# One channel block of a depthwise convolution: band products on TensorE against multiplies on ScalarE and sums on GpSimd

## Chip, cores, metric

The kernel runs on one core of a Trainium2 chip. The metric is the device time of one execution in microseconds. The names of the profile are PE (TensorE matmuls), PEld (TensorE weight loads), DVE (VectorE), ACT (ScalarE), POOL (GpSimd) and SP (SyncE, which issues the DMAs).

## What is computed

A decoder trunk of two layers over 1024 tokens of 1024 channels, all in 32-bit floats. The first layer mixes tokens with a gated causal depthwise convolution, the second with sliding-window attention; each is followed by a layer norm, a squared-ReLU MLP, another layer norm and a gated embedding. The part that matters here is the convolution:

```python
CONV_WIDTH = 31
h = x @ w_in + b_in
a, gate = jnp.split(h, 2, axis=-1)
h = a * jax.nn.sigmoid(gate)
h = lax.conv_general_dilated(          # each channel by itself: 31 taps, causal
    h, w_dw[:, None, :], window_strides=(1,), padding=[(CONV_WIDTH - 1, 0)],
    dimension_numbers=("NWC", "WIO", "NWC"), feature_group_count=D_MODEL) + b_dw
h = jax.nn.silu(layer_norm(h, ln_g, ln_b))
return h @ w_out + b_out
```

## The kernel before

Every product of two matrices is made of three TensorE products: each operand is split into a high part, rounded to a shorter format (fp32r) by a ScalarE cast, and a low remainder, formed by VectorE (`split`, `mm3`). Names ending in h and l (wh, wl, xh, xl) are these parts.

The convolution stage fills roughly the first 260 us and works by eight channel blocks of 128 channels (`c` = 0 to 7). Two generators are advanced in turn. `conv_in(c)` makes x @ w_in for the block, four steps each: it puts the sum into PSUM, takes the sigmoid of the gate on ScalarE, multiplies on VectorE and hands the gated block over to DRAM (`hand_over`, tensors zz and scr). Blocks 2 to 6 use a product with seven in place of eight parts (`conv_seven`), whose token forms T[1] to T[4] are made by `forms()` and `last_forms()`. `taps(c)` starts `LAG` = 6 steps later. It loads the block back from scr with tokens dealt into four phases (a B tile), loads the tap weights as band matrices (z, from w_dw), casts each to high and low halves (an E tile, by ScalarE and VectorE), and multiplies: per E tile nine products of 128x128 by 128x256, one for each shift. Two such tiles make a step, eight a block. The bias is added by ScalarE and the low half by VectorE (tile g), the sums are transposed on TensorE (ps slots of the kind `tr`), and the result of blocks 0 to 5 is stored to the DRAM tensor `kept`; the tiles Z[half, phase, q] (slots X and A, one for each of eight token tiles and each half of the channels) are filled from it when block 6 comes. Then `conv_ln` takes pairs of token tiles: statistics, normalization, transposition, Silu. While these last steps run, products of the embedding are woven in (`fill`). The output projection `mix_out` with w_out follows.

The order of the instructions on each engine is fixed ahead by a planner, `Recorder.schedule`. Each operation has a number by its place in the program (moved back by `later`), an estimated duration (`cost`), and is put on its engine when its operands and slots are ready, the lowest number first. `after` makes an operation wait for another; `slack` adds to the estimated ready time. Buffers come from small pools of slots by name, six PSUM slots for ps and two for tr. The planner's estimate for an addition on GpSimd is `90.0 + 2.2 * f` ns for f elements per partition; for an activation on ScalarE it is `60.0 + f * 0.85`, plus 90 for a bias pointer and 130 for a scale pointer. It also lets VectorE operations with two SBUF inputs and GpSimd operations exclude each other in time (`held`).

Of the kernel before, what the change touches and what calls it, by code (L numbers as in the profile page):

```python
# [10 lines left out]
F32 = mybir.dt.float32  # L11
F32R = mybir.dt.float32r
AF = mybir.ActivationFunctionType
ALU = mybir.AluOpType

P = 128
T = 1024
D = 1024
KB = D // P
NT = T // P  # L20
HT = 512
TAPS = 31
NH = 16
# [9 lines left out]
PH = 4  # L33
# [5 lines left out]
U = T // PH  # L39
LO = 288  # L40
LAG = 6
SC = 144
ROWS = slice(0, P // 2), slice(P // 2, P)
WAIT = 250.0
# [9 lines left out]
KEPT = 6  # L54
# [458 lines left out]
class Emit:  # L513
# [320 lines left out]

    def setup(self):
        nc, d = self.nc, self.d
        self.cc = self.const("cst", (P, 256 + NT * 32 + 2 * NH), F32)[:, 0 : 32 + 64]
        self.ident = self.const("ident", (P, P), F32)
        self.mhalf = self.const("mhalf", (P, 32), F32)[:, 0:1]
        nc.gpsimd.memset(self.mhalf, -0.5)  # L840

        self.xT = {}
        for k in ((0, 0), (0, 1), (1, 0), (1, 1)):
            for p in "hl":
                nc.slots(f"x{p}{k[0]}{k[1]}", [f"x{p}{k[0]}{k[1]}"])
            self.xT[k] = self.xT_quarter(k)
# [19 lines left out]
    def conv(self):  # L866

        nc, d, ws = self.nc, self.d, self.ws
        cc = self.cc
        ba, bg, lg, lb = (cc[:, 8 * i : 8 * i + 8] for i in range(4))  # L870
        bdw = cc[:, 32:96]
        HIGH, LOW = slice(0, P // 2), slice(P // 2, P)

        self.warm_up()
# [7 lines left out]
        Z = {}  # L882

        def hand_over(c, h, g):

            both = self.sb("wh" if (c, h) == (LAST, 1) else "zz", F32R, 2 * HT)
            self.split(g, both[:, 0:HT], both[:, HT : 2 * HT])
            if c not in scr:
                scr[c] = nc.tile(f"scr{c}", (2 * PH * P, U), F32, "DRAM")
            cols = slice(h * P, (h + 1) * P)  # L890
            dst = scr[c].scatter(lambda a: a.rearrange("(k q) u -> q k u", q=P)[:, :, cols], P, cols, 2 * PH)
            nc.sync.dma_start(dst, both.bitcast(F32).rearrange("p (k u) -> p k u", k=2 * PH))

        T = {j: [None] * 4 for j in range(1, 5)}
# [83 lines left out]
        def conv_in(c):  # L978

            if ALONE <= c < LAST:  # L980
                yield from conv_seven(c)
                return
            us = ws.get(2)
            if c == LAST:
                for kb in range(KB // 2):
                    self.load_xT(1, kb)
            for h in (0, 1) if c in (0, LAST) else (1, 0):
                pp = [self.ps() for s in range(2)]
                order = [(kb + KB // 2 * (h if c == LAST else 0)) % KB for kb in range(KB)]

                def part(s, kb):
                    wh, wl = us[kb // 4]
                    o = (kb % 4) * 256 + (1 - s) * P
                    tr = [(wh[:, o : o + P], wl[:, o : o + P], *self.xs(kb, h * HT, HT))]
                    self.mm3(pp[s], tr, kb == order[0], kb == order[-1])

                if c == 0:
                    for kb in range(KB):
                        part(0, kb)
                        part(1, kb)  # L1000
                    yield
                else:
                    for s in range(2):
                        for kb in order:
                            part(s, kb)
                        if s == 0:
                            yield
                sg = self.sb("t")
                nc.scalar.activation(sg, pp[0], AF.Sigmoid, bias=bg[:, c : c + 1], scale=1.0)
                g = self.sb("t")  # L1010
                nc.vector.scalar_tensor_tensor(
                    out=g, in0=pp[1], scalar=ba[:, c : c + 1], in1=sg, op0=ALU.add, op1=ALU.mult
                )
                hand_over(c, h, g)
                yield
            ws.done(2)

        exchange = None

        def taps(c):  # L1020

            n = SHIFTS * PH * CG
            nonlocal exchange
            for jj in range(2):
                pss = [self.ps() for k in range(2)]
                for j in range(2):
# [4 lines left out]
                    src = scr[c].scatter(  # L1031
                        lambda a, pair=pair: a.rearrange("(k p j) u -> (k p) j u", p=CG, j=NG)[:, pair, :], P, slice(0, U), 2
                    )
                    nc.sync.dma_start(G2[:, :, HIST : HIST + U], src)
                    exchange = nc.ops[-1]
                    for k in range(2):
                        w = nc.tile("z", (P, n))
                        nc.sync.dma_start(w, d["w_dw"][c, jj, 2 * j + k])
                        w = w.rearrange("p (m q) -> p m q", q=PH * CG)
# [3 lines left out]
                        if e in fresh:  # L1043
# [4 lines left out]
                            out=ev[HIGH, :, 1, :], in0=w[HIGH], in1=ev[HIGH, :, 0, :].bitcast(F32), op=ALU.subtract  # L1048
                        )
                        for i in range(SHIFTS):  # L1050
                            o = k * LO + HIST - i
# [6 lines left out]
                y = self.sb("g")  # L1058
                for k in range(2):
                    r = slice(k * P // 2, (k + 1) * P // 2)  # L1060
                    for j in range(2):
                        half = slice(j * U, (j + 1) * U)
                        b = 4 * c + 2 * jj + j
# [5 lines left out]
                pt = self.ps("tr")  # L1069
                pv = pt.rearrange("p (h f j k q) -> p h j k f q", h=2, f=PH, j=2, k=2)  # L1070
                nc.slack = SLACK
                for h in range(2):
                    for j in range(2):
                        o = h * P + j * U
                        nc.tensor.transpose(pv[:, h, j], y[:, o : o + P], self.ident)
                nc.slack = 0.0
                if c < KEPT:
                    for h in range(2):
                        if jj == 0:
                            wait[h] = self.sb("t")  # L1080
                        v = wait[h].rearrange("p (f j u) -> p f j u", f=PH, j=2)
                        src = pt[:, h * 256 : (h + 1) * 256].rearrange("p (f u) -> p f u", f=PH)
                        (nc.scalar.copy if h else nc.vector.tensor_copy)(v[:, :, jj, :], src)
                        if jj:
                            dst = kept.rearrange("p (s c u) -> p s c u", s=2 * PH, c=KEPT)
# [3 lines left out]
                if c == KEPT and jj == 0:  # L1089
                    for q in range(2):  # L1090
                        m = min(4, KEPT - 4 * q)
                        for h in range(2):
                            for f in range(PH):
                                Z[h, f, q] = self.sb("XA"[q])
                                o = ((PH * h + f) * KEPT + 4 * q) * P
                                with nc.later(BACK_BY):
                                    nc.sync.dma_start(Z[h, f, q][:, 0 : P * m], kept[:, o : o + P * m])
                for h in range(2):
                    for f in range(PH):
                        o = c % 4 * P + jj * 4 * CG  # L1100
                        dst = Z[h, f, 1][:, o : o + 4 * CG]
                        src = pt[:, (PH * h + f) * 4 * CG : (PH * h + f + 1) * 4 * CG]
# [42 lines left out]
        kept = self.dram("kept", 2 * KEPT * HT)  # L1145
        wait = {}
        stores = []
        ins = (x for c in range(8) for x in conv_in(c))
        outs = (x for c in range(8) for x in taps(c))
        for n in range(32 + LAG):  # L1150
            next(ins, None)
            if n >= LAG:
                next(outs, None)
            if n == 32:
                idle = (x[:, k, :] for q in (1, 0) for x in self.xT_quarter((q, 1), F32) for k in range(4))
                fill = self.embed(0, (0, 1), idle, lambda *v: stores.append(v))
            for k in range(WOVEN[n - 32] if n >= 32 else 0):
                next(fill)
        for g in (ins, outs):
            assert next(g, LAG) == LAG  # L1160


        with nc.later(EMBED_BY[0]):
# [10 lines left out]
        nc.move("ps", "tr")  # L1174
        with nc.after(exchange):
            gb = self.load_row("g", d["mix_g"][0:1]), self.load_row("g", d["mix_b"][0:1])
            ws.add(*[d["w_out"][0, u] for u in range(4)])
            ws.pump()
        marks = []
        for t in range(0, NT, 2):  # L1180
            conv_ln(t)
# [731 lines left out]
    def scores(self, n, g, qf):  # L1913
# [14 lines left out]

        s = nc.tile("z", (P, 4 * SC)).rearrange("p (h s) -> p h s", h=4)
        with nc.after(qf) if n == 0 else contextlib.nullcontext():  # L1930
# [118 lines left out]
def layout(a):  # L2049
    c = np.ascontiguousarray  # L2050
# [7 lines left out]
    p = np.asarray(a["p"])[:, 0]  # L2058
    r = {}
# [3 lines left out]
    r["pT"] = c(np.stack([p[0][phased], p[1]]).transpose(0, 2, 1).reshape(2, 2, P, T))  # L2063
    wi = np.asarray(a["conv_w_in"])[0]
    chan = np.arange(P).reshape(NG, CG).T.ravel()
    r["w_in"] = c(wi.reshape(2, 4, P, 2, 8, P)[..., chan].transpose(4, 0, 2, 1, 3, 5).reshape(8, 2, P, 1024))

    w2 = wi[:, np.concatenate([np.arange(D, 2 * D), np.arange(D)])].reshape(8, P, 2, 8, P)[..., chan]
    r["w_in2"] = c(w2.transpose(3, 2, 1, 0, 4).reshape(8, 2, P, 1024)[ALONE:])
# [1 line left out]
    def cm(v):  # L2071
        return v.reshape(8, P).T

    bi = np.asarray(a["conv_b_in"])[0]
    wd = np.asarray(a["conv_w_dw"])[0]
# [6 lines left out]
    for q in range(CG):  # L2082
# [5 lines left out]
    r["cconst"] = c(  # L2088
        np.concatenate(
            [  # L2090
                cm(bi[:D])[chan], cm(bi[D:])[chan],
                cm(np.asarray(a["conv_ln_g"])[0]), cm(np.asarray(a["conv_ln_b"])[0]),
                np.tile(bd, (2 * PH, 1)),
            ],
            axis=1,
        )
    )
    own = np.tril(np.ones((P, P), np.float32))
    mask = np.concatenate([own, own.T], axis=1)
    f = np.float32(THETA) ** (-np.arange(0, ROPE, 2, dtype=np.float32) / np.float32(ROPE))  # L2100
# [16 lines left out]
    wd = np.asarray(a["mlp_w_down"]).reshape(2, 8, 2, 2, P, 2, HT)  # L2117
# [16 lines left out]
```

## Time and profile before

| | |
|---|---|
| median of 3 runs | 2127.36 us (2126.59 to 2128.29) |
| profiled execution, its own time | 2126.79 us |
| span of the profile | 2124.6 us |
| granted TensorE clock | 0.999 |
| band products (ps<-B,E, 128x256) | 576 |
| instructions on GpSimd | 494 |

The page gives the busy share of every engine and the chain of work that ended last. The view by stretches gives the same for any part of the span; the view by groups puts together instructions of one engine, operation and shape, with busy time, mean duration and the idle time before them; the timeline lists instructions in order of time, where "x4" stands for four of one kind in a row, with the time from the first one's start to the last one's end. All source lines are L480, a helper's, so that instructions are told apart by their tiles.

### The profile page before, as it was taken

To read this page: it belongs to the slowest core of one execution; us is meant where nothing else is said; L and a number is where in the kernel's file an instruction comes from. 1 tells how busy PE (TensorE), PEld (TensorE's weight loads), DVE (VectorE), ACT (ScalarE), POOL (GpSimd) and SP (SyncE) were. 2 spreads that over 40 slices of the span, in tenths; PEclk is the share of its full clock that TensorE was granted. 3 is DMA by queue.
4 is the path that set the end of the run, shared out by engine and by line. 5 is a ranking of instruction groups with operands and counts; after the bars stand their busy time and mean duration, and the time that the engine had idled before them with its cause. 6 is when DMAs were issued, how large, how long until landed. Compare 5 with 4: busy or idle time off the path is not lost.

```text
span 2124.6 us, 29630 instructions
## 1 busy us (share of the span) xinstructions
PE 2110.1 (99%) x9984; PEld 1749.8 (82%) x9984; DVE 1688.8 (79%) x2692; ACT 1211.9 (57%) x2271; POOL 265.5 (12%) x494
## 2 busy tenths in 40 slices
PE   9999999999999999999999999999999999999998
PEld 7888888888888888888888878887888888888887
DVE  8767698987777879876976888698787768788688
ACT  6655654766566533344656888366666663333373
POOL 0000114100000000002131656150000000000041
PEclk9999999999999999999999999999999999999999
DMA  7768964887787757564586112677877785574735
GB/s 258 235 213 285 290 202 151 290 268 249 263 263 262 262 157 249 184 197 155 174 305 220 48 54 93 216 248 246 273 260 262 269 310 174 184 247 164 244 110 203
DMA packets 220760, 463.99 MB, mean 218 GB/s; under 512 B 22208, under 2 KB 55616, under 8 KB 220608
## 3 DMA queue, kind: packets, MB, share of 16 engines
q1 hardware_dynamic: 220608, 462.11, 64.9%
q8 instruction: 78, 1.28, 0.2%
q14 instruction: 74, 0.61, 0.1%
HBM read 314.96 MB, written 147.06 MB: 217 GB/s over the span
## 4 chain that ended last, share of the span: by engine, by line
PE 86%; DVE 6%; ACT 3%; DMA 3%; issue 1%; POOL 1%; SPq 0%; DVEq 0%; POOLq 0%; ACTq 0%
PE ps L480 66%; PE tr L480 20%; ACT z L480 2%; DVE z L480 1%; DMA raw<-in_w_up_dram 1%; DVE t L480 1%; DVE g L480 1%; DVE sm L480 1%; POOL sm L480 1%; DVE wl L480 1%; DVE B L480 1%; DVE E L480 0%; DMA wh<-gate_t 0%; DVE xl L480 0%; DMA hid<-zz 0%
## 5 line engine op out<-in xcount | busy, mean ns | idle before, releaser
L480 PE MATMUL ps<-xh 128*128 128x512 f32 x618 | 240.4, 389 | 0.0
L480 PE MATMUL ps<-xl,xh 128*128 128x512 f32 x618 | 240.4, 389 | 0.0
L480 PE MATMUL ps<-xh,xl 128*128 128x512 f32 x618 | 240.4, 389 | 0.0
L480 POOL TENSOR_SCALAR sm<-sm 128x1 f32<-128x1 f32 x72 | 26.4, 370 | 1371.3 <-DVE E L480 609.2
L480 PE MATMUL ps<-xh,wh 128*128 128x512 f32 x496 | 193.6, 394 | 1.9 <-ACT z L480 1.9
L480 PE MATMUL ps<-xl,wh 128*128 128x512 f32 x496 | 194.4, 392 | 0.0
L480 PE MATMUL ps<-xh,wl 128*128 128x512 f32 x496 | 194.1, 392 | 0.0
L480 ACT CAST wh<-raw 128x1024 fp32r<-128x1024 f32 (+2 forms) x134 | 119.4, 895 | 92.8 <-PE ps L480 65.6
L480 ACT CAST xh<-wh 128x1024 fp32r<-128x1024 f32 x76 | 79.7, 1049 | 119.0 <-PE ps L480 81.2
L480 DVE TENSOR_TENSOR wl<-raw,wh 128x1024 fp32r<-128x1024 f32 (+2 forms) x100 | 97.9, 981 | 54.3 <-ACT wh L480 53.9
L480 PEld LDWEIGHTS ps<-xh,xl 128*128 128x128 f32 x618 | 116.0, 188 | 24.2
L480 PEld LDWEIGHTS ps<-xl,xh 128*128 128x128 f32 x618 | 116.0, 188 | 24.1
L480 PEld LDWEIGHTS ps<-xh 128*128 128x128 f32 x618 | 116.0, 188 | 23.9
L480 ACT CAST wh<-g 128x512 fp32r<-128x512 f32 x136 | 81.0, 619 | 92.9 <-PE ps L480 61.0
L480 PE MATMUL ps<-wh,xh 128*128 128x512 f32 (+1 forms) x304 | 119.1, 392 | 0.6 <-DMA wh<-gate_t 0.6
L480 PE MATMUL ps<-wl,xh 128*128 128x512 f32 (+1 forms) x304 | 119.2, 392 | 0.0
L480 PE MATMUL ps<-wh,xl 128*128 128x512 f32 (+1 forms) x304 | 119.1, 393 | 0.0
L480 DVE TENSOR_TENSOR wl<-g,wh 128x512 fp32r<-128x512 f32 x136 | 90.0, 688 | 34.7 <-ACT wh L480 34.5
L480 ACT ACTIVATE t<-t 128x512 f32<-128x512 f32 x144 | 91.0, 632 | 44.1 <-DVE t L480 42.2
L480 PEld LDWEIGHTS ps<-xh,wh 128*128 128x128 f32 x496 | 93.6, 189 | 22.5 <-ACT z L480 2.3
L480 PEld LDWEIGHTS ps<-xh,wl 128*128 128x128 f32 x496 | 93.6, 189 | 19.6
L480 PEld LDWEIGHTS ps<-xl,wh 128*128 128x128 f32 x496 | 93.8, 189 | 18.4 <-DVE xl L480 0.5
(418 smaller groups left out, 5748.3 us busy)
## 6 DMA issues: line engine op xcount, KB each, us to landing
wh<-hid SPq DMA_DIRECT2D x78, 512.0 KB, 4.3
raw<-in_w_up_dram SPq DMA_DIRECT2D x68, 512.0 KB, 4.3
wl<-in_w_down_dram SPq DMA_DIRECT2D x58, 512.0 KB, 4.8
hid<-zz SPq DMA_DIRECT2D x96, 256.0 KB, 4.8
z<-in_w_dw_dram SPq DMA_DIRECT2D x64, 288.0 KB, 4.0
hid<-t SPq DMA_DIRECT2D x64, 256.0 KB, 4.8
raw<-hid SPq DMA_DIRECT2D x30, 512.0 KB, 4.1
hid<-z SPq DMA_DIRECT2D x36, 256.0 KB, 4.9
```

What stands on the lines that cost most here:

```text
L480: getattr(getattr(nc, o.eng), o.name)(*a, **k)
```

## The change

Channel block 0 (`OWN`) leaves the band path. Its input weights are kept in the natural order of channels, its gated values stay in natural token order in a B tile (`own`; the second token half is stored to the DRAM tensor `own_g` and loaded into a second B tile when needed), and for each of two token halves and two pairs of phases, 31 ScalarE activations multiply the shifted tokens by one tap each (the first adds the bias), into two buffers in turn; GpSimd adds them up. The four results are transposed on TensorE; two go to `kept` as before, and the two of the second half are copied from PSUM directly into their Z tiles, whose loads then leave out block 0's columns. The multiplies are recorded from step 11 on at 4.75 to a step. In addition, the four loads of w_out are put in as two pairs, the second 70 numbers later.

```diff
+OWN = 0
+OWN_FROM, OWN_RATE = 11, 4.75
+OWN_LAST = (1, 0), (1, 2)
+OWN_LAG, OWN_ASK, OWN_NEXT = 6, 22, 12
+OWN_SLACK = 3000.0
+OUT_BY = 70
...
     def conv(self):
...
-                g = self.sb("t")
+                if c == OWN:
+                    if h == 0:
+                        own[0] = nc.tile("B", (P, 2 * LO))
+                        g = own[0][:, TAPS - 1 : TAPS - 1 + HT]
+                    else:
+                        g = self.sb("t")
+                    rows, g = g, g.rearrange("p (u f) -> p f u", f=PH)
+                    sg, pp[1] = (v.rearrange("p (f u) -> p f u", f=PH) for v in (sg, pp[1]))
+                else:
+                    g = self.sb("t")
                 nc.vector.scalar_tensor_tensor(
                     out=g, in0=pp[1], scalar=ba[:, c : c + 1], in1=sg, op0=ALU.add, op1=ALU.mult
                 )
-                hand_over(c, h, g)
+                if c == OWN:
+                    if h == 0:
+                        nc.gpsimd.memset(own[0][:, 0 : TAPS - 1], 0.0)
+                    else:
+                        own[1] = self.dram("own_g", HT)
+                        nc.sync.dma_start(own[1], rows)
+                else:
+                    hand_over(c, h, g)
...
+        def taps_alone():
+            n = PH // 2 * P
+            acc, part = self.sums[:, 0:n], nc.tile("z", (P, 2 * LO))
+            part = [part[:, k * n : (k + 1) * n] for k in range(2)]
+            pend = []
+            def give(h, f, y):
+                pt = self.transpose4([y[:, k * P : (k + 1) * P] for k in range(2)], OWN_SLACK)[:, 0:n]
+                if (h, f) in OWN_LAST:
+                    for k, copy in enumerate((nc.vector.tensor_copy, nc.scalar.copy)):
+                        copy(Z[h, f + k, 0][:, OWN * P : (OWN + 1) * P], pt[:, k * P : (k + 1) * P])
+                    return
+                v = self.sb("t")[:, 0:n]
+                nc.scalar.copy(v, pt)
+                dst = kept.rearrange("p (s c u) -> p s c u", s=2 * PH, c=KEPT)
+                nc.sync.dma_start(dst[:, PH * h + f : PH * h + f + 2, OWN, :], v.rearrange("p (f u) -> p f u", f=2))
+            for h in range(2):
+                near = own[h]
+                for f in range(0, PH, 2):
+                    for i in range(TAPS):
+                        src = near[:, i : i + HT].rearrange("p (u f) -> p f u", f=PH)[:, f : f + 2, :]
+                        w = own_taps[:, i : i + 1]
+                        out = part[i % 2] if i else acc
+                        bias = dict(bias=own_bias) if i == 0 else {}
+                        with nc.after(T[3][3][1]) if (h, f, i) == (0, 0, 0) else contextlib.nullcontext():
+                            nc.scalar.activation(out.rearrange("p (f u) -> p f u", f=2), src, AF.Identity, scale=w, **bias)
+                        if i:
+                            if i == OWN_ASK:
+                                pend.append((h, f, self.sb("g")[:, 0:n]))
+                            to = acc if i < TAPS - 1 else pend[0][2]
+                            nc.gpsimd.tensor_tensor(out=to, in0=acc, in1=out, op=ALU.add)
+                        yield
+                        if (h, f, i) == (0, 2, OWN_NEXT):
+                            half, own[1] = own[1], nc.tile("B", (P, 2 * LO))
+                            nc.scalar.copy(own[1][:, 0 : TAPS - 1], near[:, HT : HT + TAPS - 1])
+                            nc.sync.dma_start(own[1][:, TAPS - 1 : TAPS - 1 + HT], half)
+                        if i == OWN_LAG and pend:
+                            give(*pend.pop())
+            give(*pend.pop())
...
         def taps(c):
+            if c == OWN:
+                for k in range(4):
+                    yield
+                return
...
+                                b = P if q == 0 and (h, f // 2 * 2) in OWN_LAST else 0
                                 with nc.later(BACK_BY):
-                                    nc.sync.dma_start(Z[h, f, q][:, 0 : P * m], kept[:, o : o + P * m])
+                                    nc.sync.dma_start(Z[h, f, q][:, b : P * m], kept[:, o + b : o + P * m])
...
+            made += OWN_RATE if n >= OWN_FROM else 0
+            while made >= 1:
+                next(alone, None)
+                made -= 1
...
-            ws.add(*[d["w_out"][0, u] for u in range(4)])
-            ws.pump()
+            for k in range(2):
+                ws.add(*[d["w_out"][0, 2 * k + u] for u in range(2)])
+                with nc.later(OUT_BY * k):
+                    ws.pump()
```

The rest of the change carries the taps and the bias of block 0 into the constants (`cconst`, `cc`), gives the running sum `acc` a place in the same constant tile (`self.sums`), and orders the weights `w_in` of block 0.

More of the change, by code (lines that the diff above doesn't have):

```diff
@@ L836, in setup @@
         nc, d = self.nc, self.d
-        self.cc = self.const("cst", (P, 256 + NT * 32 + 2 * NH), F32)[:, 0 : 32 + 64]
+        cst = self.const("cst", (P, 256 + NT * 32 + 2 * NH), F32)
+        self.cc, self.sums = cst[:, 0 : 32 + 64 + TAPS + 1], cst[:, 32 + 64 + TAPS + 1 :]
         self.ident = self.const("ident", (P, P), F32)
@@ L871, in conv @@
         bdw = cc[:, 32:96]
+        own_taps, own_bias = cc[:, 96 : 96 + TAPS], cc[:, 96 + TAPS : 97 + TAPS]
+        own = {}
         HIGH, LOW = slice(0, P // 2), slice(P // 2, P)
@@ L1149, in conv @@
         outs = (x for c in range(8) for x in taps(c))
+        alone = taps_alone()
+        made = 0
         for n in range(32 + LAG):
@@ L1160, in conv @@
             assert next(g, LAG) == LAG
+        for k in alone:
+            pass
         with nc.later(EMBED_BY[0]):
@@ L2065, in layout @@
     chan = np.arange(P).reshape(NG, CG).T.ravel()
-    r["w_in"] = c(wi.reshape(2, 4, P, 2, 8, P)[..., chan].transpose(4, 0, 2, 1, 3, 5).reshape(8, 2, P, 1024))
+    order = np.tile(chan, (8, 1))
+    order[OWN] = np.arange(P)
+    order += np.arange(8)[:, None] * P
+    r["w_in"] = c(wi.reshape(2, 4, P, 2, D)[..., order].transpose(4, 0, 2, 1, 3, 5).reshape(8, 2, P, 1024))
     w2 = wi[:, np.concatenate([np.arange(D, 2 * D), np.arange(D)])].reshape(8, P, 2, 8, P)[..., chan]
@@ L2090, in layout @@
             [
-                cm(bi[:D])[chan], cm(bi[D:])[chan],
+                bi[:D][order].T, bi[D:][order].T,
                 cm(np.asarray(a["conv_ln_g"])[0]), cm(np.asarray(a["conv_ln_b"])[0]),
                 np.tile(bd, (2 * PH, 1)),
+                np.concatenate([wd[:, OWN * P : (OWN + 1) * P], np.asarray(a["conv_b_dw"])[0][None, OWN * P : (OWN + 1) * P]]).T,
             ],
```

## The prediction

> **What bounds the kernel now.** I read the page's busy shares and its chain first, then the busy time in stretches of the convolution stage, then the waits of TensorE there.
>
> ```profile
> PE 2110.1 (99%) x9984; PEld 1749.8 (82%) x9984; DVE 1688.8 (79%) x2692; ACT 1211.9 (57%) x2271; POOL 265.5 (12%) x494
> PE 86%; DVE 6%; ACT 3%; DMA 3%; issue 1%; POOL 1%; SPq 0%; DVEq 0%; POOLq 0%; ACTq 0%
> 51.00:60.00 9.00, 9.00 (x60) 8.19 (x60) 7.81 (x12) 4.80 (x10) 0.22 (x2) 1.00 0.86 255
> 60.00:70.00 10.00, 9.07 (x53) 7.69 (x51) 9.41 (x17) 6.47 (x12) 1.26 (x3) 1.00 0.71 216
> 70.00:250.00 180.00, 179.95 (x1049) 158.44 (x1050) 123.90 (x190) 106.89 (x201) 4.31 (x27) 1.00 0.79 248
> 250.00:262.00 12.00, 12.00 (x67) 10.14 (x67) 8.81 (x21) 8.29 (x20) 2.98 (x5) 1.00 1.07 358
> 262.00:291.00 29.00, 29.00 (x158) 23.70 (x158) 27.74 (x61) 20.22 (x39) 12.41 (x20) 1.00 0.75 262
> PE ps L480 <- DVE E L480: 1.0, 2, 0.6
> ```
>
> TensorE is busy 99% and the chain lies on it for 86%. In the stretches (columns: length, then PE, PEld, DVE, ACT, POOL busy, granted clock, DMA) it has 0.05 us of idle time in 70 to 250 us, at a clock of 1.00. A matmul taken away there is therefore time taken away, as long as the engines that prepare its operands keep up. The one place where they don't is 60 to 70 us: VectorE is busy 9.41 of 10 us and TensorE idles 0.93 us, in two waits for a band tile (E). In 51 to 60 us VectorE is busy 87% and TensorE never waits. I use these two rows as my scale for what a nearly full helper engine costs TensorE.
>
> **What is removed.** Block 0's band products: 2 halves of its channels x 2 x 2 groups x 9 shifts = 72 matmuls of the 576.
>
> ```profile
> 61.31 1.23 PE L480 MATMUL ps<-B,E 128*128 128x256 f32 x8 [0.58 <-DVE E L480]
> 70.05 1.32 PE L480 MATMUL ps<-B,E 128*128 128x256 f32 x9 [0.39 <-DVE E L480]
> 90.24 2.31 PE L480 MATMUL ps<-B,E 128*128 128x256 f32 x18
> 92.39 0.63 PE L480 MATMUL ps<-A,wh 128*128 128x512 f32 x2
> L480 DVE TENSOR_TENSOR E<-z,E 64x576 fp32r<-64x576 f32 x56 | 41.6, 754 | 32.0 <-ACT E L480 26.8 <-DMA B<-scr 3.8 <-PE ps L480 0.6
> L480 DVE TENSOR_TENSOR g<-g,ps 64x512 f32<-64x512 f32 x28 | 19.3, 691 | 1.9 <-ACT g L480 1.1
> L480 DVE TENSOR_TENSOR t<-t,ps 128x512 f32<-128x512 f32 x14 | 9.6, 685 | 3.7 <-PE ps L480 3.0 <-ACT t L480 0.7
> L480 DVE COPY t<-tr 128x256 f32<-128x256 f32 x11 | 4.6, 422 | 1.9 <-PE tr L480 1.7
> L480 ACT CAST E<-z 128x576 fp32r<-128x576 f32 x54 | 35.6, 667 | 6.3 <-PE ps L480 3.2 <-DMA z<-in_w_dw_dram 1.6 <-ACT A L480 0.6
> L480 ACT ACTIVATE g<-ps,cst 64x256 f32<-64x256 f32 x56 | 24.7, 466 | 19.9 <-PE ps L480 19.1
> L480 ACT COPY t<-tr 128x256 f32<-128x256 f32 x11 | 4.1, 369 | 3.5 <-DVE t L480 3.4
> ```
>
> Eighteen of them run from 90.24 to the next product at 92.39: 2.15 us, 0.119 us each. 72 x 0.119 = 8.6 us off TensorE. The eight transposes of the block's sums are replaced by eight of the same shape: nothing. Both waits for E (0.58 and 0.39 us) stand between block 0's own bands, the first to be made, so up to 1.0 us goes with them. What is late next there: channel block 2's token forms and weight splits, which TensorE now reaches some 6 us earlier; but VectorE is rid of block 0's work in the same stretch, so I count the whole 1.0.
>
> VectorE loses 8 band remainders (0.74), 4 sums from PSUM (0.69) and 2 copies (0.42): 9.5 us, 8 of it after 51 us. ScalarE loses 8 band casts (0.66), 8 evictions (0.44) and 2 copies (0.37): 9.5 us, about 8 after 51 us. SP loses 8 band loads, 4 loads of the exchanged block and 2 stores to it, and gets one store and one load of block 0's second half; block 0's stores to `kept` stay two. That is 12 issues less on its queue, nothing on the path.
>
> **What is added.** 4 chains (two token halves x two phase pairs) of 31 multiplies on ScalarE and 30 adds on GpSimd, each 128x256: 124 and 120. The trace has neither form, so I bound them by neighbours.
>
> ```profile
> 266.06 1.93 ACT L480 ACTIVATE t<-tr,cst 128x256 f32<-128x256 f32 x4
> 361.24 2.94 ACT L480 ACTIVATE z<-B,sm 128x512 f32<-128x512 f32 x4 [1.89 <-DVE sm L480]
> 1074.48 1.29 POOL L480 TENSOR_TENSOR B<-B,t 128x512 f32<-128x512 f32 x1 [5.27 <-DMA X<-in_w_q_dram]
> 1091.08 1.67 POOL L480 TENSOR_TENSOR E<-E,t 128x512 f32<-128x512 f32 x1 [1.92 <-DVE t L480]
> 1165.02 0.19 POOL L480 COPY z<-cst 128x4 f32<-128x4 f32 x1
> 362.86 6.43 POOL L480 TENSOR_TENSOR B<-z,g 128x512 f32<-128x512 f32 x4 [1.33 <-DVE z L480]
> 362.09 4.81 DVE L480 TENSOR_TENSOR z<-z,g 128x512 f32<-128x512 f32 x4 [0.37 <-ACT z L480]
> 282.05 1.24 DVE L480 TENSOR_TENSOR E<-E,bo 128x512 f32<-128x512 f32 x2
> 50.34 0.69 DVE L480 TENSOR_TENSOR X<-g,X 128x512 fp32r<-128x512 f32 x1
> 268.65 0.77 POOL L480 TENSOR_SCALAR A<-A,sm 128x512 f32<-128x512 f32 x1
> 265.05 0.64 DVE L480 BATCH_NORM_STATS2 sm<-X 128x6 f32<-128x512 f32 x1
> L480 DVE BATCH_NORM_STATS2 sm<-X 128x6 f32<-128x512 f32 x6 | 4.0, 684 | 1.3 <-DMA X<-kept 1.3
> 290.85 29.26 PE ps L480 x129
> raw<-in_w_up_dram SPq DMA_DIRECT2D x68, 512.0 KB, 4.3
> ```
>
> *ScalarE.* Four 128x256 activations with scale and bias pointers take 1.93 us, 0.48 each; a plain 128x256 copy 0.37. The multiply has a scale pointer and, but for four, no bias pointer: 0.37 to 0.48, I take 0.45. 124 x 0.45 = 56 us. ScalarE's free time from 51 us (the gate: the split at 50.34, the last of the third token form) to 262 us is 211 - 126.5 = 84.5 us by the stretches; the stage is 8.6 us shorter and 8 us of block 0's work is gone, so 84 us stay. ScalarE goes from 60% to (126.5 - 8 + 56) / 202 = 86%. It fits.
>
> *GpSimd.* An add of 512 takes 1.29 us alone and 1.67 beside VectorE; 0.19 us of an instruction is fixed by the 128x4 copy, so 256 take 0.19 + 1.10 / 2 = 0.74 alone, and 0.93 in company. 120 x 0.93 = 112 us from 51 us on: the chain could end at 163 us and, stretched by ScalarE's other work, somewhere about 200. The second token half is first wanted by the fifth tile's normalization, at 268.65. GpSimd does next to nothing else there (4.31 of 180 us). So neither engine's sum decides.
>
> *What they do to VectorE.* In the layer norm, four VectorE products with two SBUF inputs take 4.81 us beside GpSimd's adds and 0.62 each elsewhere: 2.3 us lost to three adds (6.43 us for four, 1.61 each), 0.78 per add of 512, so by 0.74 / 1.29 about 0.45 per add of 256. 120 x 0.45 = 54 us in which such a VectorE operation must wait. VectorE's own load from 51 to 262 us is 149.9 - 8 = 142 us, of which at least 29 (the sums g and t from PSUM, 19.3 + 9.6) have one SBUF input and, I assume, run beside GpSimd. 142 - 29 + 54 = 167 of 202 us: 83% of the shared path, less than the 87% at which TensorE did not wait.
>
> [...]
>
> *Stalls of TensorE.* Bounds: none (the 51 to 60 us row) and 0.93 per 10 us (the 60 to 70 us row) over 202 us, 19 us. Loads of 83% and 86% lie near the first row; I take 0.1 per 10 us, 2 us in all.
>
> *The order in the queues.* A multiply waits for the add two before it (two buffers). ScalarE runs in order, so behind a waiting multiply stand the band casts and the gates' sigmoids, and behind those VectorE's remainders and TensorE. The planner's own price for the add (its formula is in the code) is 0.65 us, and it puts the multiplies where nothing of earlier number is ready; a real 0.93 makes the queue wait some of the time. That is in the 2 us.
>
> *The boundary to the layer norm.* The four tiles of the second half get block 0's 128 columns late, by a copy from PSUM; six of the eight first-half statistics (the x6 row is of 70 to 250 us) are done early now, so at least two and at most four move behind block 0's end: up to 4 x 0.64 us, perhaps on the VectorE that is busy 27.74 of 29 us from 262 us on, plus four short copies. TensorE has the woven embedding products as cover. Bounds 0 and 3 us; I take 1. Splitting the w_out loads in two moves half of them later; their products begin only with the long run at 290.85, so I count nothing. If a unit came late, TensorE would wait a part of a load's 4.3 us. The store and load of block 0's second half, some 4.3 us each, are hidden by the first two chains, 62 multiplies; late, they would hold ScalarE's queue.
>
> **Sum.** -8.6 - 1.0 + 2.0 + 1.0 = -6.6 us. The profiled execution took 2126.8 us (span 2124.6), 0.6 us under the median of 2127.4; so 2120.2 on its scale, 2120.8 on the median's. I say 2120.5. With the stalls between 0 and 5 us the forecast's own range is 2117 to 2123. About 0.2% (4.3 us) is what a measurement of this kernel can tell from no change, so faster means below 2123.1.
>
> **Rivals.**
>
> *The shared path is nearly full.* If an add closes it for longer than my 0.45, up to 0.74, VectorE is as loaded as in 60 to 70 us for part of the stage. For: GpSimd's adds run up to a third longer beside VectorE. Against: VectorE idles 56 us of 180 now, mostly because its buffers are full. A third of the stage at 0.93 per 10 us is 6.3 us: 2126.8 - 9.6 + 6.3 + 1 = 2124.5, no change to be told.
>
> *ScalarE becomes the bound: slower.* The multiplies read every fourth element, a step of 16 bytes; no row of this trace has such a read. 512 against 256 elements cost (2.94 - 1.93) / 4 = 0.25 us, so if the step halves the rate, the multiply costs 0.45 + 0.25 = 0.70 us and 124 of them 87 us, where 84 are free. The point from which this decides is 84 / 124 = 0.68 us. A full ScalarE, in order, would hold TensorE up as a full VectorE does in 60 to 70 us: 0.93 per 10 us over 202 us, 19 us; 2126.8 - 9.6 + 19 = 2136. Against: nothing in the rows, only that the price must rise by half. [...]
>
> **Chances.** Forecast 0.62; shared path 0.20; ScalarE bound 0.18. I leave the step of 16 bytes that little because even at half rate the demand only just exceeds the free time and the multiplies may run past 262 us for the last chain. The range takes the forecast's whole range, the shared-path case and the lower part of the ScalarE case: 2116.5 to 2129. Faster 0.62, same 0.20, slower 0.18.
>
> **What would show it.** Right: 504 band matmuls, TensorE's busy time lower by about 8.6 us, no wait for E in 60 to 70 us, multiplies of 0.4 to 0.5 us and adds of 0.7 to 1.0 us, the last add before 262 us, ScalarE about 86% busy. Wrong: multiplies of 0.7 us or longer (second rival), VectorE's band remainders well above 0.75 us with TensorE waiting for E or wl (first rival), or TensorE waiting in 262 to 291 us for the second half's tiles.

## The result: slower by 0.61%

The changed kernel takes 2140.41 us (median of 4 runs, 2138.27 to 2141.59) against 2126.98 us for the kernel before on the same chip: ratio 1.0061, 95% interval 1.0044 to 1.0078. The forecast was 2120.5 us in a range of 2116.5 to 2129; what came is the rival "ScalarE becomes the bound", priced at 2136. The profiled execution has a span of 2139.9 us, 15.3 us more than before.

The page of the changed kernel (busy time, then shares of the chain), and its stretches (length, then PE, PEld, DVE, ACT, POOL busy, granted clock, DMA):

```profile
PE 2108.3 (99%) x9912; PEld 1743.1 (81%) x9912; DVE 1694.2 (79%) x2678; ACT 1284.5 (60%) x2380; POOL 375.6 (18%) x611
PE 77%; ACT 8%; DVE 5%; DMA 4%; issue 2%; POOL 2%; SPq 0%; POOLq 0%; DVEq 0%; ACTq 0%
51.00:262.00 211.00, 197.34 (x1083) 168.62 (x1083) 145.86 (x201) 190.47 (x330) 113.47 (x149) 0.98 0.70 214
262.00:291.00 29.00, 27.19 (x153) 22.88 (x152) 25.84 (x57) 22.54 (x47) 10.43 (x20) 1.00 0.97 348
291.00:320.00 29.00, 27.63 (x137) 22.74 (x136) 25.12 (x48) 11.67 (x23) 7.33 (x4) 1.00 0.44 140
```

The 72 matmuls are gone (9984 to 9912), but TensorE's busy time fell by only 1.8 us and its idle time rose from 14.5 to 31.6 us (span less busy). Of that rise of 17.1 us, 12.7 lie in 51 to 262 us (13.66 us idle there; before, 0.98 by its four stretches), 3.2 in 262 to 320 us (1.81 + 1.37; none before in 262 to 291), and the other 1.2 elsewhere. In 51 to 262 us ScalarE is busy 190 of 211 us; it was 126. The chain lies on ScalarE for 8%, before for 3%.

What TensorE waits for up to 330 us (total, times, longest), and the new groups with two of VectorE's (busy, mean ns of one, idle before):

```profile
PE ps L486 <- ACT t L486: 9.9, 5, 3.3
PE tr L486 <- DVE g L486: 1.9, 3, 1.2
PE ps L486 <- DVE xh L486: 1.8, 1, 1.8
PE tr L486 <- POOL A L486: 1.4, 1, 1.4
PE ps L486 <- DVE E L486: 1.2, 2, 0.7
L486 ACT ACTIVATE z<-B,cst 128x256 f32<-128x256 f32 x120 | 88.3, 758 | 7.8 <-POOL cst L486 6.3 <-DVE E L486 0.6
L486 DVE TENSOR_TENSOR E<-z,E 64x576 fp32r<-64x576 f32 x56 | 48.6, 875 | 25.5 <-ACT E L486 25.3
L486 DVE TENSOR_TENSOR g<-g,ps 64x512 f32<-64x512 f32 x28 | 19.3, 690 | 9.8 <-ACT g L486 9.2
L486 POOL TENSOR_TENSOR cst<-cst,z 128x256 f32<-128x256 f32 x116 | 105.8, 912 | 67.1 <-ACT z L486 57.0 <-ACT cst L486 4.6
```

The multiply takes 0.758 us from its start to its end and 88.3 / 120 = 0.736 us of busy time; I had taken 0.45, and named 0.68 as the point from which ScalarE decides. VectorE's band remainders (E), which have two SBUF inputs, went from 754 to 875 ns, while its sums g, with one input from PSUM, stayed at 691 and 690. The largest wait is the one for t, which ScalarE writes from PSUM. One case of it, in the timeline of ScalarE and TensorE:

```profile
94.83 0.66 ACT L486 CAST E<-z 128x576 fp32r<-128x576 f32 x1
95.39 1.42 ACT L486 ACTIVATE z<-B,cst 128x256 f32<-128x256 f32 x2
96.83 0.47 ACT L486 ACTIVATE g<-ps,cst 64x256 f32<-64x256 f32 x1
97.33 0.62 ACT L486 CAST wh<-g 128x512 fp32r<-128x512 f32 x1
97.97 0.47 ACT L486 ACTIVATE g<-ps,cst 64x256 f32<-64x256 f32 x1
98.46 0.62 ACT L486 CAST wh<-g 128x512 fp32r<-128x512 f32 x1
98.99 0.68 ACT L486 ACTIVATE t<-ps,cst 128x512 f32<-128x512 f32 x1
99.72 0.80 PE L486 MATMUL ps<-xh,wh 128*128 128x512 f32 x1 [2.85 <-ACT t L486]
```

ScalarE takes its instructions in the planner's fixed order and is busy 4.74 of the 4.84 us from 94.83 to 99.67; the t that frees TensorE stands behind casts, evictions and two multiplies. TensorE starts when t is written, 2.85 us late. The length of the multiplies is not all of it. Shortly before, ScalarE had stood at a multiply that waited for an add, and ahead of the t that ended the longest wait (3.29 us, to 165.37) it had stood for a load of band weights:

```profile
92.59 0.76 ACT L486 ACTIVATE z<-B,cst 128x256 f32<-128x256 f32 x1 [1.06 <-POOL cst L486]
162.41 0.67 ACT L486 CAST E<-z 128x576 fp32r<-128x576 f32 x1 [1.28 <-DMA z<-in_w_dw_dram]
```

### The profile page after: what moved, and what is told of

Read it like the earlier page. It is cut to its first block, busy times and chain, and to the rows that moved or that the text cites. A ratio compares the mean times of both kernels' runs of the same rounds, so it can differ in the third digit from the quotient of the medians.

```text
span 2139.9 us, 29734 instructions
## 1 busy us (share of the span) xinstructions
PE 2108.3 (99%) x9912; PEld 1743.1 (81%) x9912; DVE 1694.2 (79%) x2678; ACT 1284.5 (60%) x2380; POOL 375.6 (18%) x611
## 4 chain that ended last, share of the span: by engine, by line
PE 77%; ACT 8%; DVE 5%; DMA 4%; issue 2%; POOL 2%; SPq 0%; POOLq 0%; DVEq 0%; ACTq 0%
PE ps L486 59%; PE tr L486 18%; ACT z L486 3%; POOL cst L486 1%; ACT t L486 1%; ACT wh L486 1%; ACT g L486 1%; ACT E L486 1%; DVE sm L486 1%; DVE t L486 1%; DVE z L486 1%; DVE wl L486 1%; DVE g L486 1%; DMA t<-proj 0%; DVE xl L486 0%
## 5 line engine op out<-in xcount | busy, mean ns | idle before, releaser
L486 PE MATMUL ps<-xh 128*128 128x512 f32 x636 | 247.4, 389 | 0.0
L486 PE MATMUL ps<-xl,xh 128*128 128x512 f32 x636 | 247.4, 389 | 0.0
L486 PE MATMUL ps<-xh,xl 128*128 128x512 f32 x636 | 247.4, 389 | 0.0
L486 PE MATMUL ps<-xh,wh 128*128 128x512 f32 x484 | 190.0, 396 | 10.2 <-ACT t L486 9.9
L486 PE MATMUL ps<-wh,xh 128*128 128x512 f32 x412 | 162.4, 395 | 4.2 <-DMA wh<-gate_t 2.4
L486 PE MATMUL ps<-wh,xl 128*128 128x512 f32 x412 | 162.8, 396 | 0.0
L486 PE MATMUL ps<-wl,xh 128*128 128x512 f32 x412 | 162.8, 395 | 0.0
L486 POOL TENSOR_TENSOR cst<-cst,z 128x256 f32<-128x256 f32 x116 | 105.8, 912 | 67.1 <-ACT z L486 57.0
L486 DVE TENSOR_TENSOR xl<-wh,xh 128x1024 fp32r<-128x1024 f32 x76 | 92.9, 1223 | 21.0 <-ACT xh L486 20.6
```

Of the source, the lines that this page charges most:

```text
L486: getattr(getattr(nc, o.eng), o.name)(*a, **k)
```

## Experiments

Three theories, named as in the expectations. **A**: the multiplies read with a step of 16 bytes and are slow for that, ScalarE is full, and TensorE waits behind it. **B**: the multiply's price is that of its scale pointer or of the engine, not of the step. **C**: GpSimd's adds hold up VectorE's operations with two SBUF inputs, and VectorE is late. The first five kernels issue on every engine the same order of instructions as the changed kernel, so only durations differ.

Each measured time is followed by its ratio to the kernel before, run on the same chip, with the 95% interval. The chips differ a little (the kernel before has medians from 2125.07 to 2126.98 us on them), so it is the ratios that are compared.

**1. Successive elements.** The multiplies read the wrong elements, 256 in a row.

```diff
-src = near[:, i : i + HT].rearrange("p (u f) -> p f u", f=PH)[:, f : f + 2, :]
+src = near[:, i : i + n].rearrange("p (f u) -> p f u", f=2)
```

> The multiplies read 256 successive elements (values wrong) in place of every fourth of 512; the order of all instructions on every engine is that of the changed kernel. Theory A (the step of 16 bytes slows the read, ScalarE is full, TensorE waits for it): the multiply falls from 0.76 us to about 0.52 us in the listing, ScalarE's busy time from 51 to 262 us falls by some 28 us, TensorE's waits for ScalarE's t go, the time falls to 2118 to 2124 us. Theory B (the price is the scale pointer's or the engine's own, not the step's): 0.76 us stays and the time stays at 2140 us. Theory C (GpSimd's adds shut VectorE out): the multiply may get cheaper but the time stays above 2132 us.

**2. A step of 8 bytes** in place of 16.

> The multiplies read every second element of 512 (a step of 8 bytes, values wrong), same order of all instructions. [...] If any step above one element costs, it stays at 0.65 to 0.76 us and the time above 2132 us.

Measured: 2128.24 us, 1.0018 (1.0008 to 1.0027), and 2127.49 us, 1.0015 (1.0005 to 1.0024). The groups of the first (three rows), and the multiply of the second:

```profile
L486 ACT ACTIVATE z<-B,cst 128x256 f32<-128x256 f32 x120 | 59.0, 507 | 18.8 <-POOL cst L486 17.7 <-DVE E L486 0.7
L486 DVE TENSOR_TENSOR E<-z,E 64x576 fp32r<-64x576 f32 x56 | 52.5, 946 | 20.2 <-ACT E L486 19.9
PE ps L486 <- ACT t L486: 5.9, 3, 2.8
```
```profile
L486 ACT ACTIVATE z<-B,cst 128x256 f32<-128x256 f32 x120 | 61.6, 529 | 18.6 <-POOL cst L486 17.2 <-DVE E L486 0.7
```

The step alone makes the multiply 0.758 in place of 0.507 us; 8 bytes cost next to nothing (0.529). That confirms A's price and rules out B: 0.43% between the ratios of the changed kernel and of experiment 1, 9 us. But I had expected 2118 to 2124. With fast multiplies ScalarE now stands 17.7 us in front of multiplies that wait for an add, and remainders take 0.946 us. Something of C is there too.

**3, 4, 5. Adds on 16 columns, multiplies on 16 columns, both** (the last add and the first three multiplies of a chain stay whole; the planner goes on charging 256 columns, so the order stays).

```diff
-nc.gpsimd.tensor_tensor(out=to, in0=acc, in1=out, op=ALU.add)
+nc.gpsimd.tensor_tensor(out=to[:, 0:16], in0=acc[:, 0:16], in1=out[:, 0:16], op=ALU.add)
...
-nc.scalar.activation(out..., src, AF.Identity, scale=w, **bias)
+nc.scalar.activation(out[:, 0:16], src[:, 0, 0:16], AF.Identity, scale=w, **bias)
```

> All but the last add of each chain work on 16 of 256 columns (sums left out, values wrong); multiplies as in the changed kernel, same order. Theory A: adds fall from 0.91 to about 0.25 us, VectorE's band remainders go back from 0.875 to 0.755 us, but ScalarE stays full: the time falls by 0 to 4 us, to 2136 to 2140. Theory C (shared path decides): the time falls to 2118 to 2126 us.

> All but the first three multiplies of each chain work on 16 of 256 columns (values wrong); adds as in the changed kernel, same order. Theory A: multiplies of about 0.27 us, ScalarE no longer full, TensorE's waits for ScalarE's t go: 2118 to 2124 us, with VectorE's band remainders still at 0.85 us or more. Theory C: VectorE and GpSimd still in each other's way, the time stays above 2132 us.

> Multiplies (but the first three of a chain) and adds (but the last) both on 16 columns, the order of all instructions that of the changed kernel. If the rest of the loss is the helpers' work, TensorE's stalls between 60 and 250 us are gone and only those of the order remain (about 3.2 us at the layer norm, 0.6 us at the start): 2119 to 2121 us. If the fixed order by itself costs more, it stays above 2123 us.

| ratio to before (95%) | adds whole | adds of 16 columns |
|---|---|---|
| multiplies whole, step 16 bytes | 1.0061 (1.0044 to 1.0078) | 1.0038 (1.0023 to 1.0053) |
| multiplies of 16 columns | 1.0002 (0.9993 to 1.0012) | 0.9982 (0.9973 to 0.9991) |

Remainders in the kernel with short adds, then in the one with short multiplies, then TensorE's stretch with both short:

```profile
L486 DVE TENSOR_TENSOR E<-z,E 64x576 fp32r<-64x576 f32 x56 | 42.1, 758 | 25.3 <-ACT E L486 25.1
```
```profile
L486 DVE TENSOR_TENSOR E<-z,E 64x576 fp32r<-64x576 f32 x56 | 54.0, 973 | 20.6 <-ACT E L486 20.5
```
```profile
51.00:262.00 211.00, 208.23 (x1187) 181.42 (x1186) 147.73 (x238) 156.83 (x357) 58.28 (x161) 1.00 0.79 246
```

The two costs add up almost without interplay. Whole multiplies cost 0.59 or 0.56% (12 us) by the columns of the table, whole adds 0.23 or 0.20% (4 to 5 us) by its rows. A is the larger by far; my expectation that the time would stay at 2136 to 2140 us without the adds (2132.84 came, 2135.1 by its ratio) was wrong, if narrowly, and so was that short multiplies alone would bring 2118 to 2124 (2125.58). Stretched remainders belong to the adds: 758 ns without them, 973 with them.

**6. The ceiling.** Only 3 of the 31 taps of each chain; the planner orders anew.

> Each chain has three taps (first, second, last) in place of 31; the others are left out of the program, and the planner orders the rest anew. This is the removal of the band products alone: 8.6 us of products and up to 1.0 us of waits less, 2116 to 2119 us. If the time stays above 2122 us, a part of the loss is neither the multiplies nor the adds but the missing band work itself (another order at the layer norm).

Measured: 2120.33 us, 0.9978 (0.9968 to 0.9988). Its page, its stretches in 51 to 291 us, and the waits of 51 to 330 us of more than 0.3 us:

```profile
PE 2099.9 (99%) x9912; PEld 1740.2 (82%) x9912; DVE 1679.5 (79%) x2678; ACT 1212.0 (57%) x2268; POOL 275.4 (13%) x499
51.00:262.00 211.00, 209.68 (x1200) 183.09 (x1199) 150.93 (x247) 135.64 (x255) 23.45 (x57) 1.00 0.81 255
262.00:291.00 29.00, 27.18 (x142) 22.34 (x140) 24.75 (x47) 16.37 (x33) 7.67 (x4) 1.00 0.52 183
PE ps L486 <- DVE xh L486: 1.2, 1, 1.2
285.58 0.55 PE L486 MATMUL tr<-ident,A 128*128 128x128 f32 x3 [1.82 <-POOL A L486]
```

The bands' 10.2 us of busy time are gone, but even with next to no helper work only 4.7 us of gain remain (2116 to 2119 us were expected): the boundary to the layer norm loses 3.0 us in two waits, for xh just ahead of 262 us and for A, where the kernel before had none. The same place in the changed kernel:

```profile
284.64 0.50 PE L486 MATMUL ps<-wh,xh 128*128 128x512 f32 x1 [1.81 <-DVE xh L486]
302.12 4.98 POOL L486 TENSOR_SCALAR A<-A,sm 128x512 f32<-128x512 f32 x1 [1.03 <-issue]
302.94 3.69 DVE L486 TENSOR_TENSOR E<-E,bo 128x512 f32<-128x512 f32 x6
307.15 0.55 PE L486 MATMUL tr<-ident,A 128*128 128x128 f32 x3 [1.37 <-POOL A L486]
```

A normalization on GpSimd that takes about 0.8 us elsewhere (0.821 on average in kernel 10) takes 4.98 us beside six VectorE adds with two SBUF inputs, and TensorE waits for its tile A.

**9, 10. The last pair of tiles normalized on VectorE**, in the changed kernel and in the one with 3 taps.

```diff
-(nc.gpsimd if q else nc.vector).tensor_scalar(out=z[q]
+(nc.gpsimd if q and t0 < 6 else nc.vector).tensor_scalar(out=z[q]
```

> The changed kernel, but the last pair of token tiles of the layer norm is normalized on VectorE instead of one of the two on GpSimd (the instruction that took 4.98 us). If the wait of 1.4 us for A at the boundary comes from that instruction alone: 1 to 2 us less than the changed kernel, 2138 to 2139.5, and no wait of TensorE for a GpSimd tile A. If the boundary is late because the woven products run out or VectorE is full there: no difference within 0.5 us. In both cases the multiplies stay at 0.75 us and ScalarE at about 190 of 211 us.

> The kernel with 3 of 31 taps in a chain (28 multiplies and 28 adds of each chain left out), with the same move to VectorE. If the GpSimd normalization causes the boundary's loss: its wait of 1.8 us for A goes, and the time is 1.4 to 1.8 us under that kernel's 2120.3, at 2118.5 to 2119. If not: 2120.3 within 0.5 us.

Measured: 2136.48 us, 1.0052 (1.0039 to 1.0066); and 2117.08 us, 0.9959 (0.9946 to 0.9971). The 3-tap kernel's GpSimd normalizations and its boundary:

```profile
L486 POOL TENSOR_SCALAR A<-A,sm 128x512 f32<-128x512 f32 x6 | 4.9, 821 | 0.3 <-issue 0.2
262.00:291.00 29.00, 28.53 (x147) 23.73 (x148) 26.80 (x52) 17.06 (x34) 1.72 (x4) 1.00 0.54 183
```

In both, the wait for A is gone from the list. By the ratios the 3-tap kernel gains 0.19%, 4 us, where I expected 1.4 to 1.8; the intervals just overlap, and of the 4.1 us less idle time in its trace 1.8 are this wait and 1.1 lie in 700 to 1100 us, which the edit doesn't touch. The trace's 1.8 us is the better figure. The changed kernel gains 0.09%, with intervals that overlap widely: its time shows no more than a direction.

**7, 8, 11. Whole convolutions with other orders.** Kernel 7 keeps block 0's values in four phase planes so that every multiply reads successive elements (a fourth of them falls into two pieces of 128), with the planner's prices at 0.49 and 0.74 us. Kernel 8 is the changed kernel with prices 0.66 and 0.74. Kernel 11 is 7 with earlier multiplies, an earlier hand-over of each chain's sum and the last pair on VectorE. The lines after the dots are kernel 11's alone.

```diff
+nc.price = dict(scalar=490.0, gpsimd=740.0)
+at, a = divmod(i - (TAPS - 1) + f, PH)
+pl = planes(near)
+srcs = [(slice(0, 2), pl[:, a : a + 2, at + PAD : at + PAD + P])]    # a < PH - 1
...
-OWN_FROM, OWN_RATE = 11, 4.75
+OWN_FROM, OWN_RATE = 7, 4.0
-OWN_LAG, OWN_ASK, OWN_NEXT = 6, 22, 12
-OWN_SLACK = 3000.0
+OWN_LAG, OWN_ASK, OWN_NEXT = 3, 20, 4
+OWN_SLACK = 1000.0
```

> Same sums as the changed kernel, but block 0's gated values lie in four phase planes, so that every multiply reads successive elements (a quarter of them as two of 128); the planner charges 0.49 us for a multiply and 0.74 us for an add. Theory A: multiplies of about 0.51 us (0.39 for 128 columns), ScalarE some 85% busy, 2120 to 2127 us. If GpSimd's adds are the rest of the loss, VectorE's band remainders stay at 0.93 us or more and the time is in the upper half of that.

> The changed kernel with its step of four elements, but the planner charges what the trace shows (0.66 us for a multiply, 0.74 us for an add) in place of 0.41 and 0.65. If the queue's order is the loss (multiplies that wait at the head of ScalarE's queue), the time falls to 2124 to 2130 us. If ScalarE's capacity is the loss (Theory A), it stays at 2134 us or above.

> The whole convolution, block 0's values in four phase planes so that all multiplies read successive elements, the planner's prices as measured (0.49 and 0.74), the multiplies started earlier (step 7, 4 to a step), and the last pair normalized on VectorE. If what was left of the loss was the boundary and the order there: 2121 to 2124, faster than before by 0.1 to 0.25%. If the shared path of VectorE and GpSimd takes the gain whatever the order: 2125 to 2128, no change against before. Remainders of the bands 0.9 us in both.

Measured: 2126.65 us, 1.0000 (0.9991 to 1.001); 2133.82 us, 1.0032 (1.002 to 1.0044); 2126.38 us, 1.0003 (0.9994 to 1.0012). Kernel 11's stage, two groups, and the stage of kernel 8:

```profile
51.00:262.00 211.00, 205.70 (x1162) 177.50 (x1161) 166.31 (x228) 176.29 (x381) 123.78 (x155) 1.00 0.76 239
L488 DVE TENSOR_TENSOR E<-z,E 64x576 fp32r<-64x576 f32 x56 | 50.1, 904 | 17.5 <-ACT E L488 14.6 <-PE ps L488 2.7
L488 POOL TENSOR_TENSOR cst<-cst,z 128x256 f32<-128x256 f32 x116 | 114.0, 983 | 112.9 <-ACT z L488 54.6 <-ACT cst L488 53.8
```
```profile
51.00:262.00 211.00, 205.73 (x1161) 177.54 (x1160) 157.07 (x214) 198.60 (x350) 111.02 (x149) 1.00 0.76 239
```

Kernel 8 has the slow multiply and prices nearer to the trace's (its multiplies take 0.761 us, its adds 0.892). It loses 0.32% in place of 0.61, between my two branches, with intervals that just touch. So half of the loss stays, and order alone isn't it; but about half goes with the order that was planned for a multiply of 0.41 us. Nor does a busy ScalarE make the stage late by itself: it is busy 198.60 us here, more than the changed kernel's 190.47, and TensorE idles 5.27 us in the stage in place of 13.66. What kernel 8 loses besides lies behind the stage: 4.6 us of idle time in 262 to 320 us, none before. (This trace is of the fastest of six executions, 2130.48 us.)

With fast multiplies (7, 11) the whole gain of the bands is spent, and there is no difference to the kernel before. In kernel 11 TensorE idles 5.30 us in the stage (211 - 205.70), 0.98 before, and waits 2.0 us for xh behind it. Its time falls into the branch that blames the shared path, but ScalarE also stood 9.2 us in front of multiplies that waited for an add, so the time doesn't part these two. No version with the whole convolution beat the kernel before.

**12. Adds whole, but no multiply waits for one.** As 1, with every add but a chain's last reading the running sum twice. The second input is swapped only when an instruction is issued, behind the planner, so all orders are the changed kernel's.

```diff
-k = {n: ... for n, v in o.kw.items()}
+k = {n: ... for n, v in o.kw.items()}; k.pop("alone", False) and k.update(in1=k["in0"])
...
-nc.gpsimd.tensor_tensor(out=to, in0=acc, in1=out, op=ALU.add)
+nc.gpsimd.tensor_tensor(out=to, in0=acc, in1=out, op=ALU.add); nc.ops[-1].kw["alone"] = i < TAPS - 1
```

> Contiguous multiplies at full length and adds at full length, in the changed kernel's order, but all adds of a chain except the last read the running sum twice instead of the multiply's result: GpSimd does the same work and no multiply waits for an add any more. In the kernel with contiguous multiplies ScalarE stood 17.7 us at a multiply waiting for an add, TensorE waited 5.9 us for t, the ratio was 1.0018 and the remainders took 0.95 us. If the adds cost time because ScalarE, in order, stands waiting behind them: TensorE's wait for t falls to 2 us or less and the ratio to 0.998 to 1.000 (2121 to 2126). If they cost time because they stretch VectorE's band remainders: remainders stay at 0.9 us or more and the ratio stays at 1.001 to 1.002 (2127 to 2130).

Measured: 2125.8 us, 0.9998 (0.9989 to 1.0006), against 1.0018 in experiment 1.

```profile
L486 ACT ACTIVATE z<-B,cst 128x256 f32<-128x256 f32 x120 | 55.5, 503 | 0.8 <-DVE E L486 0.7
L486 DVE TENSOR_TENSOR E<-z,E 64x576 fp32r<-64x576 f32 x56 | 49.5, 889 | 20.0 <-ACT E L486 14.3 <-PE ps L486 5.2
PE ps L486 <- ACT t L486: 3.4, 2, 2.3
```

The multiplies' waits for adds are gone and 0.20%, 4 us, with them, while remainders are still stretched to 889 ns (946 in experiment 1, so some of the 4 us may be theirs). So where the multiply is fast, a large part of what the adds cost comes by way of ScalarE's queue; the wait for t fell to 3.4 us, not under 2. The 0.16% left over both parts short has intervals that touch (0.9989 and 0.9991), and how it divides between stretched remainders and the whole multiplies isn't settled.

## Why the prediction was wrong

The loss, put together from the ratios (1% is 21.3 us):

| | ratio | us |
|---|---|---|
| bands removed, wait for A mended (10 against before) | -0.41% | -8.7 |
| boundary of the layer norm (6 against 10; the trace shows 1.8 us) | +0.19% | +4.0 |
| the remaining taps' instructions, short (5 against 6) | +0.04% | +0.9 |
| adds whole (4 against 5) | +0.20% | +4.3 |
| multiplies whole, step 16 bytes (changed kernel against 4) | +0.59% | +12.5 |
| sum | +0.61% | +13.0 |

Each row is the difference of two ratios that follow on each other, so the rows add up to the measured 0.61% by construction; what they show is how it divides. Each row has an uncertainty of 0.1 to 0.2%; the small third row says only that it is small. The last row holds for the order that was planned for a multiply of 0.41 us; with the higher prices of kernel 8 the whole loss is 0.32%.

- **The removal** (-8.6 and -1.0) was right in its sum: kernel 10 has a span 10.0 us shorter (2114.6). In its parts that is luck. TensorE's busy time fell by 9.8 us (to 2100.3), where I had 8.6; the 576 band products have 75.5 us of busy time in the kernel before, 0.131 each, and 72 of these are 9.4. The waits for E went, but one of 1.2 us for xh came.
- **The multiply, 0.45 us: the step that failed.** My bounds of 0.37 to 0.48 came from rows that all read successive elements. Even for those, 0.49 of busy time came (59.0 / 120), just above both. With the step it is 0.736 of busy time, 88 us where 84 were free. In the sum this sits in the term for TensorE's stalls, which I had put at 2.0 us: idle time in the stage grew by 12.7 us. The second rival had the mechanism, its price (0.70) and the point of decision (0.68); the 19 us it gave TensorE's waits stand against 12.5 by the table, 9 of them for the step alone (experiment 1).
- **Why I gave that rival 0.18.** I wrote that nothing in the rows spoke for it but that the price must rise by half, and that a demand just above the free time would run past 262 us. Neither is a reason: no row had such a read, so no row spoke against it; and a full engine with a fixed order delays what TensorE needs now, as the rows at 95 to 99 us show (t comes 2.85 us late). What such a step costs was not shown then. The runs show it for ScalarE: the multiply takes 0.507 us on successive elements, 0.529 with a step of 8 bytes, 0.758 with 16.
- **The add, 0.93 us in company:** right (0.912), and so was that GpSimd's sum doesn't decide (113.47 of 211 us busy).
- **The shared path and the order in the queues**, together within the 2 us of stalls: too small. I compared VectorE's load with the 87% of an undisturbed stretch; kernel 11 has VectorE at 166.31 of 211 us, 79%, and TensorE idles all the same (5.30 us). The waits are for single operands, and a share of busy time doesn't show how late one of them is. The order in the queue was worth more than I allowed: up to 4 us for multiplies that stand waiting for adds, by experiment 12, and about half of the loss for an order planned with too low a price, by kernel 8.
- **The boundary, 1 us:** 3.2 us of idle time in the changed kernel, just above my bounds of 0 to 3. I had looked at the statistics on VectorE; what was late was a GpSimd normalization, beside VectorE adds, and products whose operand xh wasn't ready.
- **The clock**, which was not in the sum: next section.

## What to carry to other kernels

Price an added instruction by a row with the same access pattern; where none exists, the price has no upper bound from other rows, and the case in which the engine fills up must get a chance to match. Let the planner charge the measured price: about half of the loss went with that here. An engine that runs the bottleneck's operands in its queue is a poor place for work that fills it to nine tenths of a stage (190.47 of 211 us here), and a producer with two buffers before a slower consumer stops that queue as well (17.7 us in experiment 1). Taking away matmuls pays in full only if the stages behind them are as early as they are: kernel 6 lost 3.0 us at the layer norm.

## What the hardware showed that I had not expected

After some waits TensorE is granted half its clock (0.50). The changed kernel's stretches after the 2.85 us wait that ended at 99.72 and after one of 3.29 us that ended at 165.37, and two matmuls of the first:

```profile
100.00:103.00 3.00, 3.00 (x10) 2.41 (x11) 1.46 (x3) 2.69 (x5) 0.90 (x2) 0.50 0.19 20
103.00:106.00 3.00, 3.00 (x15) 2.47 (x14) 2.56 (x4) 2.43 (x5) 1.36 (x3) 0.99 0.69 222
168.00:170.00 2.00, 2.00 (x6) 1.52 (x6) 0.57 (x1) 1.73 (x3) 1.90 (x2) 0.50 0.80 208
100.74 0.63 PE L486 MATMUL ps<-xh,wl 128*128 128x512 f32 x1
103.41 0.39 PE L486 MATMUL ps<-xl,wh 128*128 128x512 f32 x1
```

A matmul of 128x512 takes 0.63 us there and 0.39 after it. Over 51 to 262 us the mean clock is 0.98, by my estimate about 4 us of work lost (0.02 x 211); after waits of 1.85 us (ending at 131.21) and 1.43 us (at 205.05) it stays at 1.00. It is a part of why the 9912 matmuls are busy 2108.3 us here and 2099.9 in kernel 6; the rest of those 8.4 us I can't assign.

The other kernels show that the length of a wait doesn't decide by itself. Kernel 12's stretch after a wait of 1.82 us, with the matmul that ended it, and kernel 11's after one of 2.38 us:

```profile
269.17 0.50 PE L486 MATMUL ps<-wh,xh 128*128 128x512 f32 x1 [1.82 <-DVE xh L486]
270.00:273.00 3.00, 3.00 (x12) 2.61 (x12) 3.00 (x7) 2.10 (x5) 0.00 (x0) 0.50 0.97 352
```
```profile
158.94:161.94 3.00, 3.00 (x15) 2.50 (x16) 2.94 (x6) 2.74 (x7) 1.86 (x2) 1.00 0.51 167
```

Kernel 12's wait has its twin in the changed kernel, before the same matmul (1.81 us, to 284.64), and there the clock stays at 1.00. So waits of 1.82, 2.85 and 3.29 us were followed by a clock of 0.50, and waits of 1.43, 1.81, 1.85 and 2.38 us by one of 1.00; what decides besides the length isn't shown.

And beside VectorE a GpSimd instruction was held up for longer than one VectorE instruction (0.62 us, 3.69 / 6): 0.8 us became 4.98, longer than the whole run of six VectorE adds (3.69 us).
